# One set of products for the highest channel frequency, gates of the next FFN part ahead of a part's down products, and a prelude on zeros

## The chip, the cores and the metric

The kernel runs on 1 core of one Trainium2 chip. The metric is the device time of one execution in microseconds (us), as the median of several runs. The profile is that of one further execution.

## The reference

Two transformer blocks run one after the other on 512 tokens of 1024 channels, all in float32: a first block (FFN, a mixer with a recurrence over tokens, a second FFN), then a Fourier and attention layer, then a recurrent layer. Cut to what the change touches:

```python
def swiglu(x, w_gate, w_up, w_down):
    return (jax.nn.silu(x @ w_gate) * (x @ w_up)) @ w_down     # 1024 -> 2816 -> 1024

x = x + 0.5 * swiglu(rms_norm(x, ffn1_norm), ...)
x = x + token_mixer(...)
x = x + 0.5 * swiglu(rms_norm(x, ffn2_norm), ...)
...
# Fourier branch: 4 groups of 256 channels, real part of a 2-D transform over tokens and channels
fg = f_in.reshape(b, s, 4, 256)
fmix = jnp.fft.fftn(fg, axes=(1, 3), norm="ortho").real
fmix = jnp.einsum('bsgc,gce->bsge', fmix, fourier_w)
f_out = fmix * silu(f_gate)
```

## The kernel before

**Products.** Each float32 product is made of three TensorE products on fp32r halves: a high half and a low half of either operand (`mm3`, lines 783 to 787). Activations lie with channels on the partitions, so a tile is 128 channels x 512 tokens. A weight group (`wload`, line 732) is 512 KB: a DMA into one of three buffers `raw`, a cast into one of four `wh`, and on VectorE the difference into one of four `wl`; one group feeds 24 products of 512 columns for a depth of 1024.

**Low halves put aside.** During the two FFNs `put_low` (line 760) loads weights of a later stage as well, makes their low halves and writes these to DRAM; that stage then loads them (`wload_low`) instead of working them out. Two such groups go with each of the gates 0 to 19 and one with each down product of the first two parts.

**FFN** (`ffn`, line 855). The 2816 hidden channels are 22 tiles, in three parts of 8, 8 and 6. For a tile, here called a gate, there are a gate product and an up product (48 TensorE products), then `t = pg * rstd` on VectorE, Silu on ScalarE, `u = pu * rstd` on VectorE, `u * t` on GpSimd, and the split into halves `h`, `l`. When the gates of a part are done, eight down products sum over that part's tiles (24 TensorE products each, 18 in the last part) and are added to `x`. `rstd` comes from `rms` (line 844): the halves of `x`, and `sumsq` (line 807), in which ScalarE squares and GpSimd adds.

**Fourier branch** (`_even`, lines 1395 to 1453). For each of 4 groups: two input products, a transform over the 256 channels (129 cosines and 127 sines), sums and differences of token halves `s` and `d`, their splits, and then three token transforms by `seq`, each of 12 products of 256 columns: the cosines (`c1`), the sines (`c2`), and `pn`, the cosine transform of columns 128 to 255, of which only row 0, the highest channel frequency, is used (line 1435). Two gate products of the same group follow.

**Order.** The kernel is recorded, and a planner on the host (`Rec.schedule`, line 317) puts all instructions of all engines into one order by a list of costs. Each engine, and SyncE's DMA queue, then runs its part of that order strictly. An operation's priority is its place in the program plus `bias`; `late` (60) is the bias of the sum of squares. So moving a step in the program moves its loads, its put-aside weights and its evictions in every queue. All instructions carry line 555 in the profile, the line that issues them; the names of the tiles tell them apart.

Of the kernel before, what the change touches and what calls it, by code (L numbers as in the profile page):

```python
# [8 lines left out]
F32 = mybir.dt.float32  # L9
F32R = mybir.dt.float32r  # L10
AF = mybir.ActivationFunctionType
ALU = mybir.AluOpType
# [635 lines left out]
class Net:  # L648
    def __init__(self, tc, a, ctx, wbufs=(3, 4, 4), slots=76):
        self.tc, self.a = tc, a  # L650
        self.nc = self.rec = Rec(tc.nc)
        self.cp = ctx.enter_context(tc.tile_pool(name="cst", bufs=1))
        self.wp = ctx.enter_context(tc.tile_pool(name="wgt", bufs=1))
        self.wbufs = dict(zip(("raw", "wh", "wl"), wbufs))
        self.tp = ctx.enter_context(tc.tile_pool(name="act", bufs=1))
        self.sp = ctx.enter_context(tc.tile_pool(name="small", bufs=4))
        self.pm = ctx.enter_context(tc.tile_pool(name="pmm", bufs=8, space=PSUM))
        self.dp = ctx.enter_context(tc.tile_pool(name="dram", bufs=1, space=bass.MemoryType.DRAM))
        self.n = 0
        self.slots = slots  # L660
        self.late = 60
        self.low, self.later, self.behind, self.far = {}, [], 40, None
        nc = self.nc
        self.cst = self.cp.tile([128, _NC], F32, name="cst")
        self.vec = self.cp.tile([128, _NV], F32, name="vec")
        nc.sync.dma_start(out=self.vec, in_=a["vec"])
        self.load_x(a["xT"])
        nc.sync.dma_start(out=self.cst, in_=a["cst"])
        self.ident = self.c("ident")
        self.cr = {}  # L670
        for m in ("ones", "bones"):
            self.cr[m] = self.cp.tile([128, 128], F32R, name="r" + m)
            nc.vector.tensor_copy(self.cr[m], self.c(m))
        self.eps6 = self.cst[:, _COFF["eps"]:_COFF["eps"] + 1]
        self.epsg = self.cst[:, _COFF["eps"] + 1:_COFF["eps"] + 2]
        self.one = self.cst[:, _COFF["eps"] + 3:_COFF["eps"] + 4]
# [127 lines left out]
        self.nc.vector.scalar_tensor_tensor(l, src, g, h.bitcast(F32), op0=ALU.mult, op1=ALU.subtract)  # L804
        return h, l

    def sumsq(self, gains=None):

        nc = self.nc
        acc = self.T(p="acc")  # L810
        for k in range(KT):
            if k == 0:
                q = acc
            else:
                q = self.T(p="sq")
            if gains is None:
                nc.scalar.activation(q, self.x[k], AF.Square)
            else:
                nc.scalar.activation(q, self.x[k], AF.Square, scale=gains(k))
            if k:  # L820
                nc.gpsimd.tensor_tensor(acc, acc, q, ALU.add)
        ps = self.P()
        self.fold(ps, "ones", acc)
        return ps
# [16 lines left out]
        nc.vector.tensor_scalar(r, r, -0.5 * scale, 1.5, op0=ALU.mult, op1=ALU.add)  # L841
        nc.vector.tensor_tensor(out, out, r, ALU.mult)

    def rms(self, gname):

        xs = [self.split_scaled(self.x[k], self.v(gname, k)) for k in range(KT)]
        self.rec.bias = self.late
        ps = self.sumsq()
        rstd = self.T(p="rstd")
        self.rsqrt(rstd, ps, 1.0 / D, 1e-6)  # L850
        self.rec.bias = 0
        return xs, rstd


    def ffn(self, n):
        nc = self.nc
        xs, rstd = self.rms(n + "_norm")
        g0 = 0
        for ch, nk in enumerate((8, 8, 6)):
            hs = []  # L860
            for gi in range(g0, g0 + nk):
                wg = self.group(n + "_g", gi)
                pg = self.P()
                self.gemm(pg, wg, xs)
                wu = self.group(n + "_u", gi)
                pu = self.P()
                self.gemm(pu, wu, xs)
                t = self.T()
                nc.vector.tensor_tensor(t, pg, rstd, ALU.mult)
                nc.scalar.activation(t, t, AF.Silu)  # L870
                u = self.T()
                nc.vector.tensor_tensor(u, pu, rstd, ALU.mult)
                nc.gpsimd.tensor_tensor(u, u, t, ALU.mult)
                hs.append(self.split(u))
                if gi < 20:
                    self.put_low(2)
            g0 += nk
            for m in range(8):
                wd = self.group(f"{n}_d{ch}", m)
                ps = self.P()  # L880
                self.gemm(ps, wd, hs)
                xm = self.x[m]
                nc.vector.scalar_tensor_tensor(xm, ps, 0.5, xm, op0=ALU.mult, op1=ALU.add)
                if ch < 2:
                    self.put_low(1)


    def mixer(self):
# [457 lines left out]
    def _even(self):  # L1346
        nc = self.nc
        V, G, A, PE = nc.vector, nc.gpsimd, nc.scalar, nc.tensor
# [4 lines left out]
        xs = [self.split_scaled(x[k], g12[:, k:k + 1]) for k in range(KT)]  # L1353
# [4 lines left out]
        rstd = self.T(p="rs")  # L1358
# [25 lines left out]
        for gp in range(2):  # L1384
# [7 lines left out]
            V.tensor_copy(p[0:1], fwr[0:1, 0, gs])  # L1392
            V.tensor_copy(m[0:1], fwr[0:1, 1, gs])
            fw.append((p, m))
        fo = []
        for g in range(4):
            fs = []
            for m in range(2):
                w = self.group("e_f", 2 * g + m)
                ps = self.P()  # L1400
                self.gemm(ps, w, xs)
                f = self.T()
                V.tensor_tensor(f, ps, rstd, ALU.mult)
                fs.append(self.split(f))
            pp = []
            for tp in range(2):
                ps = self.P((128, 2, 256))
                for tt in range(2):
                    sl = slice((2 * tp + tt) * 128, (2 * tp + tt) * 128 + 128)
                    for k in range(2):  # L1410
                        self.mm3(ps[:, tt], fs[k][0][:, sl], fs[k][1][:, sl], d1h[:, k], d1l[:, k], k == 0, k == 1)
                pp.append(ps)
            b = self.T(shape=(128, 2, 256))
            A.copy(b, pp[1])
            s = self.T(shape=(128, 2, 256))
            d = self.T(shape=(128, 2, 256))
            V.tensor_tensor(s, pp[0], b, ALU.add)
            V.tensor_tensor(d, pp[0], b, ALU.subtract)
            sd = (self.split(s, (128, 2, 256)), self.split(d, (128, 2, 256)))

            def seq(col, tr):
                ps = self.P((128, 2, 256))
                for e in range(2):
                    h, l = sd[e]
                    for k in range(2):
                        self.mm3(ps[:, e], h[:, k, col], l[:, k, col], d2h[tr][e][:, k], d2l[tr][e][:, k], k == 0, k == 1)
                return ps
            c1, c2 = slice(0, 128), slice(128, 256)
            pc = seq(c1, 0)
            C = self.split(pc, (128, 2, 256))  # L1430
            pq = seq(c2, 1)
            Q = self.T(shape=(128, 2, 256))
            A.copy(Q, pq)
            pn = seq(c2, 0)
            V.tensor_copy(Q[0:1], pn[0:1])
            Qs = self.split(Q, (128, 2, 256))
            fl = lambda t: t.rearrange("p e j -> p (e j)")
            if g % 2 == 0:
                (ph, pl), (mh, ml) = [self.split(t, (128, 2, 256)) for t in fw[g // 2]]
            for m in range(2):  # L1440
                wg = self.group("e_f", 8 + 2 * g + m)
                pg = self.P()
                self.gemm(pg, wg, xs)
                sg = self.T()
                V.tensor_tensor(sg, pg, rstd, ALU.mult)
                A.activation(sg, sg, AF.Silu)
                po = self.P((128, 2, 256))
                ms = slice(m * 128, m * 128 + 128)
                self.mm3(fl(po), ph[:, g % 2, ms], pl[:, g % 2, ms], fl(C[0]), fl(C[1]), True, False)
                self.mm3(fl(po), mh[:, g % 2, ms], ml[:, g % 2, ms], fl(Qs[0]), fl(Qs[1]), False, True)  # L1450
                sv = sg.rearrange("p (j e) -> p e j", e=2)
                V.tensor_tensor(sv, sv, po, ALU.mult)
                fo.append(self.split(sg))
# [283 lines left out]
    def last_norm(self, hf):  # L1737
# [4 lines left out]
        s0 = slice(256 * hf, 256 * hf + 256)  # L1742
        if hf == 0:

            w = self.sm(1, tag="fw", bufs=1)
            o = A.activation(w, self.one, AF.Sqrt)
            o.deps.append(next(p for p in reversed(self.rec.ops[:-1]) if p.table))
        acc, q7 = (self.T(shape=(128, 512), p="sq")[:, 0:256] for _ in range(2))
# [31 lines left out]
    def all(self):  # L1780
# [2 lines left out]
        mix = [("w_in", t) for t in (5, 9, 1, 6, 10, 2, 7, 11, 3, 13, 17, 21, 14, 18, 22, 15, 19, 23, *range(26, 42))]  # L1783
        mix += [("w_out_a", h) for h in range(4)] + [("w_out_b", h) for h in range(4)] + [("w_o", g) for g in range(8)]
        n = len(self.rec.ops)
        self.later = mix
        self.ffn("ffn1")

        w = [o for o in self.rec.ops[n:] if o.fn == "dma_start"][:2]
        l = [o for o in self.rec.ops[:n] if o.fn == "dma_start"]  # L1790
# [31 lines left out]
```

## Time and profile before

| | us |
|---|---|
| Runs, median of 3 (lowest, highest) | 1879.77 (1878.92, 1880.1) |
| The profiled execution | 1883.26 |
| Its span, first to last instruction | 1881.5 |
| PE busy in the span | 1842.7 |
| DVE busy | 1272.1 |
| ACT busy | 852.2 |
| POOL busy | 246.4 |

PE is TensorE's products, PEld its weight loads, DVE VectorE, ACT ScalarE, POOL GpSimd, SPq SyncE's queue that issues the DMAs. A busy time of PE counts overlapping instructions once, and says nothing on how densely they follow each other: products of 512 columns are listed as 0.39 us long and start about 0.23 us apart. The rows therefore give counts beside the times. PEclk is the granted clock of TensorE as a share of 2.4 GHz; it has two levels, 2.4 and 1.2 GHz.

### The profile page before, as it was taken

The page shows a single profiled execution, that of the slowest core. Times are in us where ns is not written, and L with a number is a line of the kernel's source. Part 1 is how long each engine was busy: PE and PEld are TensorE (multiplying, and loading weights), DVE is VectorE, ACT ScalarE, POOL GpSimd, SP SyncE. Part 2 cuts the span into 40 slices and gives each one's busy share as a digit, 9 for nine tenths or more (in the row PEclk, how much of TensorE's full clock was granted, in tenths as well). Part 3 has the DMA queues.
Part 4 walks back from the last instruction along what each step waited for, and adds up shares of the span by engine and source line. Part 5 has one row for each costly group of instructions (what it writes and reads, how often), then busy time and mean ns, then how long its engine had stood idle before and what let it go on. Part 6 is the DMA issues. An engine that isn't in the chain of part 4 may idle for free.

```text
span 1881.5 us, 26365 instructions
## 1 busy us (share of the span) xinstructions
PE 1842.7 (98%) x10324; PEld 1540.2 (82%) x10324; DVE 1272.1 (68%) x1956; ACT 852.2 (45%) x1180; POOL 246.4 (13%) x193
## 2 busy tenths in 40 slices
PE   7999999999999999999998999999999999999998
PEld 6878878887788887888887887888999888888887
DVE  7766665579857434477467567965478965899773
ACT  5333433365324333444344335422255554998771
POOL 2101100113203002211010017010000010000001
PEclk9999999999999999999999999999999999999999
DMA  7788896445533444578788773322221125556552
GB/s 249 271 302 282 293 299 201 121 152 162 179 121 112 152 137 160 197 260 308 251 281 288 252 261 107 115 66 69 90 68 59 65 79 191 178 191 211 191 179 102
DMA packets 120398, 341.10 MB, mean 181 GB/s; under 512 B 33872, under 2 KB 36176, under 8 KB 120272
## 3 DMA queue, kind: packets, MB, share of 16 engines
q1 hardware_dynamic: 120272, 339.41, 54.0%
q8 instruction: 81, 1.33, 0.3%
q14 instruction: 45, 0.37, 0.1%
HBM read 277.76 MB, written 61.60 MB: 180 GB/s over the span
## 4 chain that ended last, share of the span: by engine, by line
PE 73%; DMA 11%; DVE 11%; ACT 3%; issue 2%; POOL 0%; SPq 0%; DVEq 0%; ACTq 0%; POOLq 0%
PE pm L555 69%; DVE wl L555 5%; PE pw L555 4%; DMA low<-wl 2%; DMA raw<-o_in 2%; ACT wh L555 2%; DVE t L555 2%; DMA raw<-ffn_d 1%; DMA raw<-ffn_u 1%; DVE l L555 1%; DMA raw<-gw 1%; DMA raw<-w_in 1%; DMA raw<-w_out_a 1%; DVE wh L555 0%; DVE u L555 0%
## 5 line engine op out<-in xcount | busy, mean ns | idle before, releaser
L555 ACT CAST wh<-raw 128x1024 fp32r<-128x1024 f32 (+1 forms) x334 | 347.1, 1041 | 687.6 <-PE pm L555 278.4
L555 PE MATMUL pm<-xh,wh 128*128 128x512 f32 x1488 | 583.1, 392 | 8.4 <-ACT xh L555 8.2
L555 PE MATMUL pm<-xl,wh 128*128 128x512 f32 x1488 | 582.0, 391 | 2.5 <-DVE xl L555 2.5
L555 PE MATMUL pm<-xh,wl 128*128 128x512 f32 x1488 | 582.3, 391 | 1.1 <-DVE wl L555 1.0
L555 DVE TENSOR_TENSOR wl<-raw,wh 128x1024 fp32r<-128x1024 f32 (+1 forms) x302 | 386.3, 1282 | 202.2 <-DMA low<-wl 92.0
L555 PEld LDWEIGHTS pm<-xh,wh 128*128 128x128 f32 x1488 | 280.3, 188 | 67.2 <-ACT xh L555 9.4
L555 PEld LDWEIGHTS pm<-xl,wh 128*128 128x128 f32 x1488 | 280.4, 188 | 62.5 <-DVE xl L555 5.2
L555 PEld LDWEIGHTS pm<-xh,wl 128*128 128x128 f32 x1488 | 280.2, 188 | 60.5 <-DVE wl L555 2.8
L555 PE MATMUL pm<-h,wh 128*128 128x512 f32 (+1 forms) x832 | 319.1, 386 | 9.6 <-ACT h L555 9.0
L555 PE MATMUL pm<-l,wh 128*128 128x512 f32 (+1 forms) x832 | 319.9, 385 | 1.1 <-DVE l L555 1.1
L555 PE MATMUL pm<-h,wl 128*128 128x512 f32 (+1 forms) x832 | 319.5, 385 | 1.4 <-DMA wl<-low 1.2
L555 POOL TENSOR_TENSOR t<-t,t 128x512 f32<-128x512 f32 x60 | 88.8, 1481 | 932.1 <-DVE t L555 712.5
L555 PEld LDWEIGHTS pm<-h,wh 128*128 128x128 f32 x832 | 157.4, 190 | 42.8 <-ACT h L555 10.5
L555 PEld LDWEIGHTS pm<-l,wh 128*128 128x128 f32 x832 | 157.9, 190 | 33.7 <-DVE l L555 3.5
L555 PEld LDWEIGHTS pm<-h,wl 128*128 128x128 f32 x832 | 157.8, 190 | 32.1 <-DMA wl<-low 1.6
L555 DVE TENSOR_TENSOR t<-pm,rstd 128x512 f32<-128x512 f32 x146 | 98.8, 685 | 22.1 <-PE pm L555 17.6
L555 ACT ACT_TABLE_LOAD x71 | 91.1, 1283 | 24.8 <-DVE s L555 15.7
L555 DVE CAST wh<-raw 128x1024 fp32r<-128x1024 f32 x74 | 53.9, 728 | 58.2 <-PE pm L555 31.1
L555 POOL TENSOR_TENSOR acc<-acc,sq 128x512 f32<-128x512 f32 x42 | 66.2, 1584 | 140.0 <-ACT sq L555 139.7
L555 DVE TENSOR_TENSOR x<-x,pm 128x512 f32<-128x512 f32 (+1 forms) x44 | 27.9, 637 | 72.5 <-PE pm L555 70.4
L555 ACT ACTIVATE t<-t 128x512 f32<-128x512 f32 x100 | 59.7, 626 | 21.7 <-DVE t L555 20.1
L555 DVE TENSOR_TENSOR l<-t,h 128x512 fp32r<-128x512 f32 x87 | 61.0, 709 | 6.9 <-ACT h L555 5.5
(251 smaller groups left out, 2040.1 us busy)
## 6 DMA issues: line engine op xcount, KB each, us to landing
low<-wl SPq DMA_DIRECT2D x106, 512.0 KB, 3.8
wl<-low SPq DMA_DIRECT2D x106, 512.0 KB, 3.5
raw<-w_in SPq DMA_DIRECT2D x76, 512.0 KB, 4.7
raw<-o_in SPq DMA_DIRECT2D x64, 512.0 KB, 4.5
raw<-ffn_g SPq DMA_DIRECT2D x44, 512.0 KB, 4.4
raw<-ffn_u SPq DMA_DIRECT2D x44, 512.0 KB, 5.1
raw<-ffn_d SPq DMA_DIRECT2D x32, 512.0 KB, 5.1
raw<-o_out SPq DMA_DIRECT2D x32, 512.0 KB, 4.5
```

The source lines that it names most:

```text
L555: o.ins = getattr(getattr(self.nc, o.eng), o.fn)(*o.args, **o.kw)
```

## The change

There are four edits.

- Before anything else a tile `z` is zeroed on GpSimd, ScalarE takes a square root of one of its columns, and TensorE multiplies `z` by itself 20 times (128x512) into a tile that nobody reads. The tag of a one-column tile in `last_norm` is renamed so that it has a buffer of its own.
- In the first FFN, the seven additions of the sum of squares go from GpSimd to VectorE, and the bias of that sum from 60 to 100.
- In both FFNs, gate 8 comes ahead of the eight down products of the first part, gate 16 ahead of the first six of the second part, and the other two of the second part come behind gate 21, ahead of those of the third part.
- In the Fourier branch, all four groups go through input products, channel transform and splits first. Column 128 of each group's halves is copied into columns 0, 32, 64 and 96 of two zeroed tiles `ny`, and 12 products on these give `pn` for all groups at once; ScalarE copies it to SBUF. The other two token transforms and the gates follow group by group.

```diff
@@ Net.__init__ @@
+        z = self.T(F32R, p="z")
+        nc.gpsimd.memset(z.bitcast(F32), 0.0)
+        nc.scalar.activation(self.sm(1, tag="fw", bufs=1), z[:, 0:1].bitcast(F32), AF.Sqrt)
+        ps = self.P()
+        for _ in range(20):
+            nc.tensor.matmul(ps, z[:, 0:128], z, start=True, stop=True)
@@ sumsq @@
-                nc.gpsimd.tensor_tensor(acc, acc, q, ALU.add)
+                getattr(nc, adds).tensor_tensor(acc, acc, q, ALU.add)
@@ ffn @@
-        xs, rstd = self.rms(n + "_norm")
-        g0 = 0
-        for ch, nk in enumerate((8, 8, 6)):
-            hs = []
-            for gi in range(g0, g0 + nk):
...
-            for m in range(8):
-                wd = self.group(f"{n}_d{ch}", m)
...
+        xs, rstd = self.rms(n + "_norm", "vector" if n == "ffn1" else "gpsimd")
+        hs = [[], [], []]
+        def gate(gi):
...
+        def down(ch, m):
...
+        for gi in range(22):
+            gate(gi)
+            if gi in (8, 16):
+                for m in range(8 if gi == 8 else 6):
+                    down(gi // 8 - 1, m)
+        for m in (6, 7):
+            down(1, m)
+        for m in range(8):
+            down(2, m)
@@ _even @@
+        nyq = [self.T(F32R, (128, 2, 2, 128), "ny") for _ in range(2)]
+        for t in nyq:
+            G.memset(t.bitcast(F32), 0.0)
+        sds = []
         for g in range(4):
...
+            for e in range(2):
+                for t, hl in zip(nyq, sd[e]):
+                    nc.copy(t[:, e, :, 32 * g:32 * g + 1], hl[:, :, 128:129])
+            sds.append(sd)
+        ps = self.P((128, 2, 256))
+        for e in range(2):
+            for k in range(2):
+                self.mm3(ps[:, e], nyq[0][:, e, k], nyq[1][:, e, k], d2h[0][e][:, k], d2l[0][e][:, k], k == 0, k == 1)
+        pn = self.T(shape=(128, 2, 256), p="pn")
+        A.copy(pn, ps)
+        fo = []
+        for g in range(4):
             def seq(col, tr):
...
-            pn = seq(c2, 0)
-            V.tensor_copy(Q[0:1], pn[0:1])
+            V.tensor_copy(Q[0:1], pn[32 * g:32 * g + 1])
@@ last_norm @@
-            w = self.sm(1, tag="fw", bufs=1)
+            w = self.sm(1, tag="fx", bufs=1)
@@ all @@
+        late, self.late = self.late, 100
         self.later = mix
         self.ffn("ffn1")
+        self.late = late
```

## Rows read from the trace of the kernel before

**Rows 1.** Page, part 1: busy us, share of the span, instructions.

```profile
PE 1842.7 (98%) x10324; PEld 1540.2 (82%) x10324; DVE 1272.1 (68%) x1956; ACT 852.2 (45%) x1180; POOL 246.4 (13%) x193
```

**Rows 2.** Stretches: us, busy time (xcount), PEclk, DMA share, GB/s.

```profile
0.00:21.00 21.00, 11.13 (x32) 7.15 (x33) 13.62 (x14) 13.29 (x20) 8.17 (x10) 1.00 0.73 263
106.00:118.00 12.00, 9.46 (x29) 6.90 (x28) 8.10 (x9) 4.71 (x5) 1.28 (x1) 0.72 0.90 307
118.00:243.00 125.00, 125.00 (x553) 103.56 (x552) 83.96 (x89) 46.01 (x48) 14.65 (x9) 1.00 0.85 291
243.00:248.00 5.00, 3.60 (x15) 2.42 (x14) 3.23 (x5) 3.41 (x4) 0.00 (x0) 1.00 0.72 265
1015.00:1030.00 15.00, 9.14 (x27) 6.64 (x27) 10.16 (x11) 5.78 (x7) 1.26 (x1) 0.77 0.91 305
1180.00:1400.00 220.00, 220.00 (x1251) 193.29 (x1250) 139.35 (x212) 75.56 (x103) 14.98 (x14) 1.00 0.25 83
```

**Rows 3.** Timeline of PE, first 21 us: start, length, operation, wait.

```profile
8.23 0.79 PE L555 MATMUL pm<-xh,wh 128*128 128x512 f32 x1 [8.23 <-ACT xh L555]
...
14.38 0.40 PE L555 MATMUL pm<-xl,wh 128*128 128x512 f32 x1
...
20.83 0.50 PE L555 MATMUL pm<-xl,wh 128*128 128x512 f32 x1 [1.17 <-DVE xl L555]
```

**Rows 4.** Timeline of ACT, first 21 us.

```profile
6.17 1.28 ACT L555 ACT_TABLE_LOAD   x1 [6.17 <-DMA x<-xT]
```

**Rows 5.** Timeline of DVE, first 27 us.

```profile
5.32 0.69 DVE L555 CAST wh<-raw 128x1024 fp32r<-128x1024 f32 x1 [5.32 <-DMA raw<-ffn_g]
6.05 1.22 DVE L555 TENSOR_TENSOR wl<-raw,wh 128x1024 fp32r<-128x1024 f32 x1
...
9.35 0.75 DVE L555 SCALAR_TENSOR_TENSOR xl<-x,vec,xh 128x512 fp32r<-128x512 f32 x1 [0.38 <-ACT xh L555]
...
12.25 5.46 DVE L555 SCALAR_TENSOR_TENSOR xl<-x,vec,xh 128x512 fp32r<-128x512 f32 x5
...
20.70 5.67 DVE L555 TENSOR_TENSOR wl<-raw,wh 128x1024 fp32r<-128x1024 f32 x3
```

**Rows 6.** Timeline of POOL at 242 us, the one memset of this size.

```profile
241.96 0.53 POOL L555 MEMSET z<- 128x512 f32 x1
```

**Rows 7.** Timeline of PE around 107 us, where gates end.

```profile
109.09 0.73 PE L555 MATMUL pm<-h,wh 128*128 128x512 f32 x2 [1.92 <-ACT h L555]
...
115.72 0.63 PE L555 MATMUL pm<-h,wl 128*128 128x512 f32 x1
116.15 0.62 PE L555 MATMUL pm<-h,wh 128*128 128x512 f32 x1
```

**Rows 8.** Timeline of ACT at the same place.

```profile
106.20 1.05 ACT L555 CAST wh<-raw 128x1024 fp32r<-128x1024 f32 x1 [2.46 <-DMA raw<-ffn_d]
...
108.43 0.61 ACT L555 CAST h<-t 128x512 fp32r<-128x512 f32 x1
```

**Rows 9.** Timeline of DVE around 1019 us, second FFN, second part.

```profile
1018.76 0.68 DVE L555 TENSOR_TENSOR t<-pm,rstd 128x512 f32<-128x512 f32 x1
...
1021.95 0.69 DVE L555 TENSOR_TENSOR l<-t,h 128x512 fp32r<-128x512 f32 x1
```

**Rows 10.** Timeline of PE, second FFN, where gates of the second part end.

```profile
1021.97 0.79 PE L555 MATMUL pm<-h,wh 128*128 128x512 f32 x1 [5.86 <-ACT h L555]
```

**Rows 11.** Chain that ended last, first 112 us: start, length, what.

```profile
53.84 5.21 DMA raw<-ffn_u
...
76.19 5.07 DMA raw<-ffn_u
```

**Rows 12.** Timeline of PE, Fourier branch, products of 256 columns.

```profile
1207.26 0.28 PE L555 MATMUL pm<-h,l 128*128 128x256 f32 x1
...
1210.72 0.28 PE L555 MATMUL pm<-h,l 128*128 128x256 f32 x1
```

**Rows 13.** DVE groups, 1180 to 1400 us: shape, count, busy, mean ns.

```profile
L555 DVE COPY t<-pm 1x512 f32<-1x512 f32 x4 | 2.7, 678 | 3.4 <-PE pm L555 3.4
```


## What was predicted

> **What bounds the kernel now.** I read the page's busy times first: PE is busy 1842.7 of 1881.5 us, no other engine over 68% [rows 1]. A busy PE can still be slow, so I counted products by stretch next; in those rows the first bracket is PE's count, and the last three values are PEclk, DMA share and GB/s [rows 2]. From 118 to 243 us 553 products of 512 columns start in 125.00 us: 0.226 us each. I take this as PE at its peak and price every stretch by it; what is over is time that an edit can give back. Three kinds of place show an excess:
>
> - The first 21 us: 32 products are 7.2 us of work, so 13.8 us are lost. The timeline of PE tells why: the first product starts at 8.23 and lasts 0.79, at 14.38 one lasts 0.40. So the engine is idle for 8.2 us, on the lower of its two levels for about 6 us after its first product, and at the end waits for `xl` [rows 3].
> - The ends of the gates of a part. 106 to 118 us: 29 products, 6.55 us of work in 12, 5.4 lost. 243 to 248: 15 products, 1.6 lost. 1015 to 1030, in the second FFN: 27 products, 8.9 lost [rows 2]. PE waits there for the split of the last gate's tile (`<-ACT h`), 1.92 and 5.86 us [rows 7, 10], and then goes at the lower level: starts 0.43 us apart, PEclk 0.72 and 0.77 over the stretches [rows 2, 7].
> - In the Fourier branch there is none: PE is busy 220.00 of 220.00 us from 1180 to 1400, DVE 139, ACT 76 [rows 2]. Time is gained there only by fewer products.
>
> **The change, part by part.** The sum is made against the profiled execution, 1883.3 us (1881.5 of span and 1.8 around it); it is 3.5 us over the median of the runs, and I carry the difference over to the median.
>
> *Prelude on zeros.* The memset costs POOL 0.53 us [rows 6], so the 20 products can start at about 1.2 us. No row shows a prelude; the nearest is the first stretch, where the level rose about 6 us after the first product [rows 3]. By it 14 products go 0.43 us apart (7.2 us by the clock) and six at 0.226 (1.4), and the first real product starts at 8.5, at the upper level. It was 8.23 before, so the idle time stays and what goes is the slow part: 8.5 us lost instead of 13.8, 5.3 gained. The square root pulls the table load of 1.28 us, which waited for the first DMA of `x` and held up the first `xh` [rows 4], into idle time; behind the prelude this is worth nothing. If the level rises at once, the first real product can start at 8.23 - 1.28 = 6.95 and 6.8 us are gained; if it doesn't rise in the prelude, PE is taken until 1.2 + 20 x 0.43 = 9.8, 1.6 us later than before, and 1.6 is lost.
>
> *Additions to VectorE.* While GpSimd adds, VectorE's own work is stretched: five `xl` take 5.46 us, against 0.75 for a lone one; three `wl` 5.67, against 1.22 for a lone one [rows 5]. The seven additions at 0.69 us, the length of a difference of the same size [rows 9], cost VectorE 4.8 us ahead of the next weights. VectorE's work until the third of these `wl`: 1.9 for the first weights, eight `xl` at 0.75, a second `wl` 1.2, additions 4.8, three `wl` 3.7, with two small casts some 18 us from 5.3: 23.3 if nothing else makes it idle, where it was 26.4 [rows 5]. So the weights come 3.1 us earlier, PE 5.3. The weights have nothing to spare: the second down weight of the first part, eighteen groups on, is cast from 106.20 to 107.25, and PE had done with the first one at 107.17 [rows 7, 8]. The start is therefore worth between 3.1 (stream without slack) and 5.3. I take 4.0, ends -1.6 and 6.8 from above.
>
> *Gates between gates and down products.* Removed: the wait for the last gate's split. In its place PE has another gate, 48 products or 10.9 us, and then the 21 products of a down product that don't need the last tile, 4.8 us: 15.6 us of cover. What has to fit: from the end of the last up product to the end of `l`. At the worst end that product's end lies 21 products ahead of the stall: 1021.97 - 5.86 - 0.2 - 4.75 = 1011.2; `t` left PSUM only at 1018.76, because VectorE's strict order held it behind `wl`, and `l` ended at 1022.6 [rows 9, 10]: 11.5 us, under the cover. With each moved gate go its two weight loads, two put-aside groups with their writes, and its evictions, ahead of eight (six) down weights on SP's queue and VectorE. Per PE time a gate and two down products ask the same of both: 3.1 MB of DMA per 10.9 us, 289 GB/s at 0.524 MB a transfer. The trace holds 291 GB/s at a DMA share of 0.85 with PE at its peak for 125 us [rows 2]. So I count 1.5 of 1.6, 8.5 of 8.9, and at the first end, where the weights too were late, 4.0 of 5.4: 14.0. Ends: 9.5 (the first end gives nothing, 0.5 more stays at each of the others) and 16.
>
> The Trainium skill's page "TensorE: Matmul & The Clock Gate" (HAM oscillation) warns of idle gaps, but only of longer ones than the 1.92 us here. By it the first end would have cost its 1.9 us of idle time alone, and the forecast would be 2.1 us later; the rows show the lower level there [rows 2, 7], so the measurement decides.
>
> *One set for the highest frequency.* Four sets of 12 products of 256 columns become one: 36 fewer. Thirty of them in a row start from 1207.26 to 1210.72, 0.119 us apart [rows 12]: 4.3 us off a busy PE. Added: 16 copies of one column per half, which no row shows. They cost no more than the one-row copy of 512, 0.68 us [rows 13], so 0 to 10.9 us, on VectorE and ScalarE, which are idle for 81 and 144 us in the stretch [rows 2]; two memsets of 0.53 on POOL and one copy on ScalarE are covered alike. Without the cover, the last group's copies (four, 2.7 us) would stand ahead of `pn`; but PE then has all other token transforms and gate products to do. The row copies stay. I take 4.2, ends 1.6 (4.3 less those 2.7) and 4.3.
>
> *All else.* The planner orders everything anew. The rest of the kernel keeps its work; I count 0, with 4 us on either side (about half of the 8.9 us stall).
>
> Sum: 4.0 + 14.0 + 4.2 = 22.2. 1883.3 - 22.2 = 1861.1 by the profile's measure, 1879.8 - 22.2 = 1857.6 by the median.
>
> **Rivals.**
>
> - *The weights set the pace of the FFNs*, and the stalls were their time to catch up. For: the chain runs through a DMA of `raw` once a gate from 53.84 to 76.19, 11.2 us a gate where PE needs 10.9 [rows 11]. 44 gates at 0.3 are 13 us back. Against: 125 us at the peak [rows 2]. Time: 1857.6 + 13 = 1871, PE waiting for `wh` or `wl` in many small gaps.
> - *The prelude doesn't do what it says*: the level stays low until real products have run. Start -1.6 instead of 4.0: 1863.
> - *Slower: evictions come too late everywhere.* In the new order a whole gate's `wl`s stand ahead of the last gate's `t` in VectorE's queue, as they did at 1018.76. It decides from 15.6 us between up product and split (11.5 was the worst). Then all six ends of parts cost 8.9: 53 us instead of the 16 of now. 1879.8 + 37 - 8.2 = 1909.
>
> **How the numbers follow.** Forecast 0.62, weights 0.22, prelude 0.08, evictions 0.08. The forecast's low end takes the best of each term and a lucky order: 6.8 + 16 + 4.3 + 4 = 31, 1849. The high end reaches to the weights' rival, 1872. About 0.2% (3.8 us) can be told from no change. Slower: the evictions and little else, 0.08. Same: the weights' rival with the low ends of start and set, 0.05. Faster: 0.87.
>
> **What would show it.** Start: a first real product near 8.5 us that lasts 0.4, and the 48th done near 20 to 21 us. Ends of parts: no `<-ACT h` wait over 1 us in either FFN, PEclk 1.00 throughout. Weights' rival: waits for `wl` or `wh` in the gates, or fewer than 440 products per 100 us. Fourier: 12 products on `ny`, 36 fewer of 256 columns, PE still without a gap. Wrong would be a new stall with PEclk at half in the mixer, or a count below the peak in the FFNs.

## The result, and the profile after

| | before | after |
|---|---|---|
| Median of the runs, us (lowest, highest) | 1879.35 (1877.19, 1880.1) | 1866.3 (1861.76, 1866.88) |
| The profiled execution | 1883.26 | 1866.76 |
| Its span | 1881.5 | 1864.9 |

The ratio of the medians is 0.993, with an interval of 0.9913 to 0.9946: faster by 13.1 us, where 22.2 were forecast. The median lies in the range (1849 to 1872), 8.7 us above the forecast of 1857.6. By the profiled executions it is 16.5 us, against the same forecast of 22.2.

First the stretches of the changed kernel that answer to [rows 2]; columns as there (the first bracket is PE's count of instructions, then PEld, DVE, ACT, POOL; the last three values are PEclk, DMA share, GB/s).

```profile
0.00:21.00 21.00, 19.10 (x70) 14.27 (x71) 14.35 (x21) 14.68 (x22) 0.73 (x5) 1.00 0.74 264
105.00:118.00 13.00, 13.00 (x59) 10.78 (x58) 7.96 (x8) 5.70 (x7) 1.30 (x1) 1.00 0.88 306
140.00:170.00 30.00, 25.79 (x110) 20.05 (x109) 13.43 (x14) 8.40 (x8) 0.00 (x0) 1.00 0.71 228
243.00:248.00 5.00, 5.00 (x24) 4.14 (x23) 4.21 (x6) 2.35 (x3) 0.15 (x1) 1.00 0.95 349
925.00:965.00 40.00, 37.90 (x165) 30.42 (x164) 23.91 (x26) 14.16 (x15) 3.42 (x2) 1.00 0.76 249
1005.00:1022.00 17.00, 17.00 (x76) 14.08 (x76) 11.26 (x14) 8.44 (x9) 1.28 (x1) 1.00 0.92 318
1055.00:1065.00 10.00, 9.28 (x41) 7.34 (x40) 5.26 (x6) 3.79 (x4) 0.00 (x0) 1.00 0.74 227
1170.00:1390.00 220.00, 220.00 (x1264) 194.17 (x1263) 143.00 (x229) 80.16 (x127) 14.45 (x14) 1.00 0.24 80
```

Read them against 0.226 us per product, as the prediction did.

- **The start.** Of the 70 products of the first 21 us 20 are the prelude, so 50 are real; before there were 32 [rows 2]. 18 x 0.226 = 4.1 us gained.
- **The old stalls are gone.** At 105 to 118, 243 to 248 and 1005 to 1022 us PE is at its peak (59, 24 and 76 products, where 57.5, 22 and 75 fit) and PEclk is 1.00. The 5.4, 1.6 and 8.9 us of [rows 2] are gained in full: 15.9.
- **There are new losses where none was before.** From 140 to 170 us 110 products begin where 132.7 fit: 5.1 us lost. From 925 to 965 it is 165 of 177, 2.7 us; from 1055 to 1065, 41 of 44, 0.7 us. Together 8.5.
- **The Fourier branch** keeps PE busy 220.00 of 220.00 us, as before, and has 36 products of 256 columns fewer, 4.3 us by [rows 12].

4.1 + 15.9 - 8.5 + 4.3 = 15.8 of the 16.6 us between the spans; 0.8 are in none of these places. All this is one execution of either kernel, and the new losses are not the same each time: in the profile of the changed kernel once more (further down) they are 2.6, 0.7 and 0.5 us at these places and 1.4 more behind 170 us, together 5.2.

What the new losses are, the waits of PE say. These rows are of the changed kernel, for 0 to 345 us (the first FFN) and 800 to 1130 us (the second): what PE waited for, us in total, times, the longest.

```profile
PE pm L555 <- DVE wl L555: 4.2, 4, 1.3
...
PE pm L555 <- DVE wl L555: 2.8, 4, 1.2
```

No wait for a split (`<-ACT h`) is left in either FFN; before it was 1.92 us at the first end and 5.86 in the second FFN [rows 7, 10], and 1.18 at 245 us. In their place PE waits for low halves of weights. PE's timeline has three of the first four, and the chain of work that ended last, from 146 to 169 us, shows what holds them up (start, length, what):

```profile
154.57 0.50 PE L555 MATMUL pm<-xh,wl 128*128 128x512 f32 x1 [1.20 <-DVE wl L555]
...
161.60 0.50 PE L555 MATMUL pm<-xh,wl 128*128 128x512 f32 x1 [1.28 <-DVE wl L555]
...
168.64 0.50 PE L555 MATMUL pm<-xh,wl 128*128 128x512 f32 x1 [1.31 <-DVE wl L555]
```

```profile
147.51 0.68 DVE x L555
148.19 1.14 DVE wl L555
149.33 0.02 issue
149.35 3.82 DMA low<-wl
...
153.29 1.24 DVE wl L555
...
162.15 1.14 DVE wl L555
163.31 3.93 DMA low<-wl
...
167.36 1.24 DVE wl L555
168.60 0.04 issue
168.64 1.43 PE pm L555 x5
```

A put-aside group takes one of the four `wl`. Its write to DRAM (`low<-wl`) takes 3.8 to 3.9 us, and only when it has landed can the next `wl` that PE needs be written into the same buffer, at 153.29 and 167.36. PE waits for those at 154.57 and 168.64. Between them, at 161.60, it waits for a `wl` begun at 160.32, which the chain puts down to a cast that was over 0.94 us before; a put-aside write issued at 156.28 would land at about 160.2 if it took the same 3.9 us (an estimate). So PE waits every 7.0 us, where 24 products take 24 x 0.226 = 5.4. The engines are not full meanwhile: DVE is busy 13.43 of the 30 us, the DMA share is 0.71. That points to a ring of waits over four buffers rather than a lack of bandwidth. The chain between 154 and 162 us also passes a load into `raw` (3.70 us) that began when the `wl` of 153.29 was done, so by itself it doesn't rule the loading out; the experiments do that.

The ring is not a steady pace of this kernel. Behind the new losses PE is at its peak again with the same four buffers (324 products, where 323 fit):

```profile
170.00:243.00 73.00, 73.00 (x324) 60.28 (x323) 48.04 (x54) 31.08 (x33) 12.85 (x7) 1.00 0.84 289
```

Why it closes at these places and not at others isn't shown.

### The profile page after: what moved, and what is told of

Its sections match the earlier page's. It is cut to its first block, busy times and chain, and to the rows that moved or that the text cites. A ratio compares the mean times of both kernels' runs of the same rounds, so it can differ in the third digit from the quotient of the medians.

```text
span 1864.9 us, 26367 instructions
## 1 busy us (share of the span) xinstructions
PE 1836.5 (98%) x10308; PEld 1535.8 (82%) x10308; DVE 1262.5 (68%) x1958; ACT 858.4 (46%) x1202; POOL 246.5 (13%) x189
## 4 chain that ended last, share of the span: by engine, by line
PE 68%; DMA 15%; DVE 10%; ACT 3%; issue 2%; POOL 1%; SPq 1%; DVEq 0%; ACTq 0%; POOLq 0%
PE pm L555 64%; DMA low<-wl 6%; DVE wl L555 6%; PE pw L555 4%; DMA raw<-o_in 2%; ACT wh L555 2%; DMA raw<-w_in 2%; DVE t L555 1%; DMA raw<-gw 1%; DMA raw<-ffn_d 1%; DMA raw<-ffn_u 1%; DMA raw<-o_out 1%; DVE l L555 1%; SPq L555 1%; DMA raw<-ffn_g 0%
## 5 line engine op out<-in xcount | busy, mean ns | idle before, releaser
L555 DVE TENSOR_TENSOR wl<-raw,wh 128x1024 fp32r<-128x1024 f32 (+1 forms) x302 | 381.3, 1264 | 203.4 <-DMA low<-wl 92.9
L555 POOL TENSOR_TENSOR t<-t,t 128x512 f32<-128x512 f32 x60 | 98.5, 1643 | 898.9 <-DVE t L555 689.9
L555 POOL TENSOR_TENSOR acc<-acc,sq 128x512 f32<-128x512 f32 x35 | 55.4, 1592 | 149.3 <-ACT sq L555 149.3
```

The costliest lines, as they stand in the source:

```text
L555: o.ins = getattr(getattr(self.nc, o.eng), o.fn)(*o.args, **o.kw)
```

## The experiments

All of them were run beside the kernel before on the same chip, whose median was 1877.89 (the first four), 1877.99 (the next four) and 1877.15 us (the last four); a chip's own difference is taken against that. The theories: that the start's lead is given back to the weight stream, so that the order alone gives nearly as much as the whole; that what limits the stream is the four `wl`, held by put-aside writes; and as rivals, that it is the loading (`raw`), the DMA bandwidth, or the put-aside groups as such. What a name or letter in a quoted expectation stands for is told there.

**The new order alone** (`ffn` of the changed kernel; no prelude, additions on GpSimd, old Fourier branch):

```diff
-        xs, rstd = self.rms(n + "_norm", "vector" if n == "ffn1" else "gpsimd")
+        xs, rstd = self.rms(n + "_norm")
```

> The kernel before with the new FFN order alone (no prelude, additions on GpSimd, bias 60, four sets for the highest frequency). In the changed kernel the order took 18.3 us of waits for the split out of the span and put 9.9 us of new waits, mostly for wl, in, at 140 to 170 and at 925 to 965 us. Theory A (the new waits come because PE now runs ahead of its weight stream, and a PE that starts 4 us later has 4 us more slack in the first FFN): the wl waits of the first FFN fall from 5.3 to 1 to 2 us, those of the second stay near 4; span 12 us below the 1881.5 of before, about 1869. Theory B (the waits belong to the order itself, whenever PE starts): 5 us of them stay in the first FFN; span near 1873, 8 us below before.

Measured: 1866.48 us, ratio 0.994 (0.9927 to 0.9954), so 11.4 of the 13 to 16 us that the whole change gives. How its first FFN stands to that of the whole shows in the count of products begun by 140, 243 and 345 us. The order alone:

```profile
0.00:140.00 140.00, 129.77 (x554) 105.08 (x555) 105.21 (x104) 58.08 (x72) 24.86 (x20) 1.00 0.80 275
0.00:243.00 243.00, 232.77 (x1009) 190.39 (x1010) 175.88 (x179) 97.58 (x113) 34.72 (x27) 1.00 0.82 283
0.00:345.00 345.00, 334.14 (x1455) 274.01 (x1456) 235.76 (x253) 128.06 (x147) 43.76 (x34) 1.00 0.77 264
```

The whole change, whose first 20 are the prelude:

```profile
0.00:140.00 140.00, 137.98 (x593) 112.36 (x594) 105.28 (x113) 60.63 (x75) 17.55 (x14) 1.00 0.83 284
0.00:243.00 243.00, 236.77 (x1024) 192.68 (x1025) 166.75 (x180) 100.11 (x116) 30.40 (x21) 1.00 0.82 279
0.00:345.00 345.00, 338.77 (x1473) 277.04 (x1474) 228.77 (x256) 131.63 (x151) 39.58 (x28) 1.00 0.78 263
```

At 140 us the whole is 573 - 554 = 19 products ahead, 4.3 us: the start's gain, intact. At 243 us it is 1004 - 1009 = 5 behind, at 345 us 2 behind. The start's lead is all given back between 140 and 243 us, in the waits for `wl`; the order alone, which comes to that place 4.3 us later, waits 0.6 us for `wl` in this FFN and not at all in the second. Two more kernels of this order with four `wl` (both further down) give the lead back at the same place: the changed kernel once more is 23 products ahead at 140 us and 3 at 243, that with 74 tiles 18 ahead and then 5 behind. So Theory A is right for the first FFN. For the second it isn't: the expectation had about 4 us of waits there for the order alone, and there is none (so its span, 1864.4 us, is below those of both theories). The waits of the second FFN vary (2.8 us in the whole change, 1.0 in its repetition, 0.3 with 74 tiles), and since the whole is level with the order alone at 345 us, the start's lead doesn't explain them; their cause is open.

**The single set alone** (the changed `_even`, nothing else):

```diff
-            pn = seq(c2, 0)
-            V.tensor_copy(Q[0:1], pn[0:1])
+            V.tensor_copy(Q[0:1], pn[32 * g:32 * g + 1])
```

> The kernel before with the Fourier edit alone. 36 products of 256 columns fewer at 0.119 us: 4.3 us off the span if PE sets the pace of the branch throughout, ratio about 0.998; PE loses under 1 us to waits between 1180 and 1400 us. Rival: the 16 column copies or the later splits hold the token transforms up, and 1 us or less is gained.

Measured: 1874.16 us, ratio 0.9977 (0.9966 to 0.9987), 3.7 us faster. The interval (2.4 to 6.4 us) holds the 4.2 of the forecast. In the changed kernel the set and its copies look thus (groups by shape, 1160 to 1400 us: count, busy us, mean ns, idle time before them):

```profile
L555 PE MATMUL pm<-h,ny 128*128 128x256 f32 x8 | 1.6, 280 | 0.0
L555 ACT CAST ny<-h 128x2 fp32r<-128x2 f32 x8 | 1.4, 192 | 0.2 <-DVE h L555 0.2
```

A copy of one column for both token halves takes 0.19 us. I had bounded it by 0.68, and nothing hung on it.

**The start alone**, and **the prelude alone** (the additions stay on GpSimd, the bias at 60):

```diff
+        z = self.T(F32R, p="z")
...
-        xs, rstd = self.rms(n + "_norm")
+        xs, rstd = self.rms(n + "_norm", "vector" if n == "ffn1" else "gpsimd")
...
+        late, self.late = self.late, 100
```

> The kernel before with the start alone: prelude, additions of the first sum on VectorE, bias 100. By 25 us PE should be 4 us ahead of before. Theory A (the weight stream of the first FFN has about 1 us of slack and decides at the first end of a part): of the 4 us 2 to 3 are left at 250 us, and the end near 107 us costs more than the 5.4 of before. Theory B (the lead is kept): 4 us off at 250 us and off the span, and the end near 107 us costs as before.

> The kernel before with the prelude on zeros alone; GpSimd still adds. If the clock's level is what the start loses, PE is 3.5 to 4.5 us ahead at 25 us as with the additions moved too. If GpSimd's additions beside VectorE hold back the xl and wl, the gain stops at 1 to 2.5 us, since at 20.83 us PE waited for xl before.

Measured: the start 1876.11 us, ratio 0.9989 (0.9975 to 1.0002); the prelude 1876.85 us, 0.9992 (0.9979 to 1.0005). Neither can be told from no change; but the intervals (from 0.4 us slower to 4.7 faster, and from 0.9 slower to 3.9 faster) don't rule out the gains of the first 21 us either. There the start alone begins 70 products, the whole of its 4.1 us, and the prelude alone 58: 38 real ones, 1.4 us more than before. This is the prelude alone, the beginning of PE's timeline and the stretch:

```profile
1.31 7.70 PE L555 MATMUL pm<-z 128*128 128x512 f32 x20 [1.31 <-POOL z L555]
8.85 0.39 PE L555 MATMUL pm<-xh,wh 128*128 128x512 f32 x1
...
0.00:21.00 21.00, 17.48 (x58) 12.61 (x59) 14.27 (x14) 14.18 (x22) 9.36 (x11) 1.00 0.74 263
```

So a third of the start's gain comes from the prelude, and two thirds come when the additions leave GpSimd and their place becomes later as well; the additions without the prelude were not run. Where the gates of the first part end, PE of the start alone waits longer than before (1.92 us [rows 7]) for the same split, but that doesn't take the lead. From 100 to 118 us 50 products begin, before 51, and by 243 us the start alone has begun 1016 - 20 = 996 real products where before began 981, 15 more or 3.4 us. First the kernel before, then the start alone:

```profile
0.00:243.00 243.00, 230.37 (x981) 187.16 (x982) 174.29 (x177) 96.62 (x112) 38.55 (x28) 0.99 0.81 280
```

```profile
0.00:243.00 243.00, 236.30 (x1016) 193.35 (x1017) 173.50 (x186) 100.77 (x117) 29.70 (x22) 0.99 0.83 286
```

That is nearer to Theory B of the expectation (the lead is kept) than to A, though in one execution, the fastest of eleven; by the median the start alone is 1.8 us faster. Its longer wait, and a later one:

```profile
106.58 0.79 PE L555 MATMUL pm<-h,wh 128*128 128x512 f32 x1 [4.17 <-ACT h L555]
...
1012.56 0.50 PE L555 MATMUL pm<-h,wh 128*128 128x512 f32 x1 [1.11 <-ACT h L555]
```

The second of these two is the place of the worst stall before, 5.86 us [rows 10]. Three kernels that keep the old order of the FFNs wait there 1.11 (the start alone), 1.58 (the prelude alone) and 4.76 us (the single set alone). So the stall is not a constant of the order.

**The changed kernel once more, and three edits of its weight stream**: a fifth `wl` (with 74 tiles of 128x512 instead of 76, to make room), a fourth `raw` instead (likewise), and no put-aside groups with the down products of the first part.

> The changed kernel once more. The ends of parts cost very different amounts from one execution to the next in the kernels with the old order (8.9 us at the second FFN's second part before, 2 to 6 us with single edits). If the wait for wl near 146 to 168 us comes from the order and the start, it stands again, 4 to 6 us, and the lead at the 48th product (9.7 us lost by then) is gone by the 1500th (16 lost). If it is chance of that execution, it is under 2 us.

```diff
-    def __init__(self, tc, a, ctx, wbufs=(3, 4, 4), slots=76):
+    def __init__(self, tc, a, ctx, wbufs=(3, 4, 5), slots=74):
```

> The changed kernel with five wl buffers for four, and 74 activation tiles for 76 to make room. Theory W (put-aside halves hold wl until they are written to DRAM, and the next wl of the FFN's own weights waits for it): the waits of PE for wl near 150 us fall from 5.3 to under 1 us, time 4 to 8 us lower, near 1860. Theory R (the raw buffers or their loads set the pace): no change in these waits. Theory D (DMA rate): no change either, DMA share above 0.85 in the stretch.

```diff
-    def __init__(self, tc, a, ctx, wbufs=(3, 4, 4), slots=76):
+    def __init__(self, tc, a, ctx, wbufs=(4, 4, 4), slots=74):
```

> The changed kernel with four raw buffers for three, and 74 activation tiles. Theory R (loads wait for a free raw): waits for wl near 150 us under 1 us, time near 1860. Theory W (wl held by put-aside writes): the waits stay at 4 us or more.

```diff
-            if ch < 2:
+            if ch == 1:
                 self.put_low(1)
```

> The changed kernel without the put-aside groups that go with the down products of the first part, in both FFNs; the eight last groups of each list make their low halves in their own stage instead. This takes the writes away where the waits are. Theory W: no wait for wl between 140 and 170 us and none of over 0.5 us between 925 and 965; time 3 to 8 us lower, less what the later stages pay. Theory R: loads are fewer as well, so the waits fall too, and only the two runs with more buffers tell W and R apart. A third cause (VectorE's own time): little change, VectorE is busy 13.4 of 30 us there.

Measured: the changed kernel 1861.99 us, ratio 0.992 (0.9907 to 0.9933); five `wl` 1855.37, 0.9881 (0.9869 to 0.9894); four `raw` 1899.1, 1.011 (1.0097 to 1.0123); fewer put-aside groups 1893.04, 1.0083 (1.007 to 1.0096).

In the changed kernel once more the waits for `wl` stand at the same place, but smaller than expected: 3.0 us in the first FFN (the expectation had 4 to 6, or under 2 if it was chance), and 121 products from 140 to 170 us instead of 110. The place is that of the order and the start; the size varies.

The stretch from 140 to 170 us with five `wl`:

```profile
140.00:170.00 30.00, 30.00 (x134) 24.85 (x133) 18.71 (x19) 13.05 (x14) 1.29 (x1) 1.00 0.91 307
```

PE is at its peak, no wait for `wl` is left in either FFN, and the DMA share rises from 0.71 to 0.91: the same weights, the same writes, 307 GB/s instead of 228. Bandwidth was there; the buffer was missing. The start's lead over the order alone is kept as well: 23 products at 140 us, 22 at 243 and 26 at 345. A fourth `raw` doesn't help but harms: PE waits for `wl` 15 times in the first FFN and 17 in the second (the row is of the whole kernel). At the old place the ring is the same: PE waits at 151.24, 158.22 and 165.13 us, 7.0 us apart, and the `wl` of 156.94 had waited 4.02 us for a put-aside write (`low<-wl`):

```profile
PE pm L555 <- DVE wl L555: 30.9, 33, 1.7
...
151.24 0.50 PE L555 MATMUL pm<-h,wl 128*128 128x512 f32 x1 [1.37 <-DVE wl L555]
...
158.22 0.50 PE L555 MATMUL pm<-xh,wl 128*128 128x512 f32 x1 [1.22 <-DVE wl L555]
```

So it isn't the loading that holds PE up there. Why more `raw` make it so much worse isn't shown by a run; that groups loaded earlier take `wl` out of turn would fit, but I didn't separate it from the different plan.

The kernel with fewer put-aside groups was meant to free the ring at its place, and did: 134 products from 140 to 170 us, at a DMA share of 0.44. But the list of groups is worked off in order, so what isn't put aside there comes later. At 337 us the ring closes again, and PE loses more than it won:

```profile
330.00:360.00 30.00, 18.71 (x61) 14.10 (x60) 11.85 (x15) 0.00 (x0) 1.29 (x1) 0.82 0.32 109
```

The chain there (start, length, what) begins like the other, with PE at its end:

```profile
337.60 1.24 DVE wl L555
338.84 0.02 issue
338.85 2.83 DMA low<-wl
...
341.78 1.24 DVE wl L555
343.02 0.04 issue
343.06 8.06 PE pm L555 x22
```

Two writes stand in it, of 2.83 and 2.92 us; from 364 us on it goes through loads into `raw` instead, so only its first part shows the mechanism at a second place. At 400 us this kernel is 114 products behind the changed one, about 26 of the 31 us between their medians. Ten groups fewer are put aside (96 writes instead of 106: two fewer in the first FFN, eight in the second); what these ten cost in their own stages isn't separated from the later place of the others.

**Controls**: 74 tiles alone; the kernel before with five `wl`; five `wl` and the new order without the start; and five `wl` with one more edit, the first sum of squares of the Fourier layer on VectorE.

> The changed kernel with 74 activation tiles for 76 and nothing else, the control of the runs with one buffer more. If the fifth wl buffer did it, the waits for wl near 150 us stand (3 to 6 us) and the time is that of the changed kernel, 1861 to 1867. If the planner's other order with 74 tiles did it, it is near 1855.

```diff
-    def __init__(self, tc, a, ctx, wbufs=(3, 4, 4), slots=76):
+    def __init__(self, tc, a, ctx, wbufs=(3, 4, 4), slots=74):
```

> The kernel before with five wl buffers and 74 tiles: old FFN order, no prelude, four sets. The late evictions at the ends of parts stood behind wl that waited for a put-aside write. Theory A (the fifth buffer alone takes most of that wait away): ends of parts cost 2 to 6 us in all instead of 16, time 1866 to 1872. Theory B (the split's own length decides, so the order is needed): 8 us or more stay, time above 1872.

```diff
 (in the kernel before)
-    def __init__(self, tc, a, ctx, wbufs=(3, 4, 4), slots=76):
+    def __init__(self, tc, a, ctx, wbufs=(3, 4, 5), slots=74):
```

> Five wl buffers, new FFN order and Fourier edit, without the prelude, with additions on GpSimd and bias 60. Theory (the start's 4 us are kept when the weight stream has slack): 4 us over the run with five buffers and the start, 1859 to 1860, with 14 us lost by the 1500th product of the first FFN instead of 9.7. Rival (the start counts nothing over the whole kernel): 1855 to 1857.

```diff
 (with five wl)
-        z = self.T(F32R, p="z")
...
-        xs, rstd = self.rms(n + "_norm", "vector" if n == "ffn1" else "gpsimd")
+        xs, rstd = self.rms(n + "_norm", "gpsimd")
...
-        late, self.late = self.late, 100
```

> Five wl buffers and the whole change, with the seven additions of the Fourier layer's first sum of squares on VectorE too. In the run with five buffers PE loses 7 us near 1146 us, most of it in a 3.4 us wait for the split of that sum and the lower level behind it. If GpSimd's additions (1.6 us each, twice seven) set that wait, it shrinks to under 2 us and the time falls by 2 to 5 us, near 1852. If the last weights or x set it, nothing changes.

```diff
 (with five wl, in _even)
-        s1 = self.sumsq()
+        s1 = self.sumsq(adds="vector")
```

Measured:

| | median, us | ratio (interval) |
|---|---|---|
| 74 tiles alone | 1863.67 | 0.9926 (0.9913 to 0.9938) |
| before with five `wl` | 1870.22 | 0.996 (0.9948 to 0.9973) |
| five `wl`, without the start | 1862.47 | 0.9919 (0.9905 to 0.9932) |
| five `wl`, sum on VectorE | 1852.94 | 0.987 (0.9856 to 0.9883) |

74 tiles change nothing: the stretch from 140 to 170 us is that of the changed kernel.

```profile
140.00:170.00 30.00, 26.25 (x113) 20.41 (x112) 13.63 (x14) 8.40 (x8) 0.00 (x0) 1.00 0.72 229
```

A fifth `wl` in the kernel before (with 74 tiles, which were not run there by themselves) takes 6.9 us off: there too buffers delayed the splits, for in the second FFN PE of this kernel waits for nothing, and at the end of the first part 0.93 us instead of 1.92. With five `wl` the start is worth 1862.47 - 1855.37 = 7.1 us by medians that stand on two chips (0.0038 by the ratios, the same); with four it could not be told from none. That is more than the 4 expected. The other way round, a fifth `wl` without the start gives nothing that the medians show: 14.7 us, where the order alone and the set alone give 11.4 + 3.7 = 15.1. Of the 7.1 us, 4.1 are the start itself. The rest stands at 118 us of the profile without the start, where the weights run short:

```profile
118.59 0.50 PE L555 MATMUL pm<-h,wh 128*128 128x512 f32 x1 [0.77 <-ACT wh L555]
...
120.11 0.50 PE L555 MATMUL pm<-h,wl 128*128 128x512 f32 x1 [0.79 <-DVE wl L555]
...
121.23 0.63 PE L555 MATMUL pm<-h,wh 128*128 128x512 f32 x1
```

From 110 to 125 us 51 products begin where 66.4 fit, 3.5 us lost. With the start 40 low halves have been begun by 118 us, without it 36, and this wait isn't there.

The last kernel is the fastest seen. Its gain over five `wl` alone, 2.4 us by medians of two chips, isn't told apart by the intervals, which overlap; the stretch from 1130 to 1165 us shows it, though, first with five `wl`, then with the sum on VectorE as well:

```profile
1130.00:1165.00 35.00, 30.13 (x121) 23.51 (x120) 30.28 (x29) 18.79 (x27) 21.88 (x12) 0.90 0.38 129
```

```profile
1130.00:1165.00 35.00, 32.52 (x135) 26.11 (x134) 32.69 (x34) 19.91 (x28) 14.79 (x8) 0.95 0.43 149
```

14 more products begin, about 3 us. The wait for the split of that sum, 3.27 us with five `wl`, is gone, as expected if GpSimd's additions set it; two waits for weights, of 1.38 and 1.10 us, stand ahead of it instead.

## Why the prediction was right and wrong

**What bounds the kernel**: right. The time came from the places that the counts had shown, and nowhere else to speak of.

**The start**: right in size, 4.1 us by the count against 4.0, for a partly wrong reason. I took the clock to rise 6 us after the first product and the first real product to begin at 8.5. In the changed kernel it begins at 7.85:

```profile
1.31 6.70 PE L555 MATMUL pm<-z 128*128 128x512 f32 x20 [1.31 <-POOL z L555]
7.85 0.39 PE L555 MATMUL pm<-xh,wh 128*128 128x512 f32 x1
```

But that decides little. In the kernel with 74 tiles it begins at 8.80 and 70 products have begun by 21 us, the same number. VectorE's chain decides, for which my working had a bound of 3.1 us, and the additions were the larger part of it. The step that failed is what follows: "the weights have nothing to spare" was said of the start, and its conclusion, that PE's lead is worth only what the stream can follow, was not carried on to 140 us, where the whole 4 us went with four `wl` in the new order.

**The ends of the gates**: the term was mis-sized, 14.0 forecast, 15.9 - 8.5 = 7.4 found. The first half was right: the wait for the last split is gone at every end, the first one included (I counted 4.0 of its 5.4), the cover was enough, and PEclk is 1.00. The step that failed is "a gate and two down products ask the same of both: 3.1 MB of DMA per 10.9 us". That compares rates, and the rates do suffice, as the 307 GB/s with five `wl` show. It leaves out for how long a transfer holds its buffer, 3.8 us of a write in which one of four `wl` is lost to PE. The peak from 118 to 243 us, on which I leant [rows 2], came behind a stall of 5.4 us that had let the stream get ahead; the order alone, 4.3 us behind the whole, and the peak behind the new losses fit that. The trace of before had a sign of it: the `wl` ahead of the late `t` of 1018.76 [rows 9], which I put down to VectorE's strict order alone, had itself waited for a put-aside write.

```profile
1017.61 1.23 DVE L555 TENSOR_TENSOR wl<-raw,wh 128x1024 fp32r<-128x1024 f32 x1 [1.85 <-DMA low<-wl]
```

With the 5.2 us of losses in the repetition the term would be 10.7, so part of the miss is the chance of one profiled execution.

**The Fourier set**: right, 4.3 us by the count and 3.7 (2.4 to 6.4) by itself.

**All else at 0**: 0.8 in the profile. The order alone, the set alone and the start alone add up to 11.4 + 3.7 + 1.8 = 16.9 us, against 13.1, 16.0 and 13.5 for the whole in three comparisons (the last with 74 tiles).

**From the profile to the median**: I carried a difference of 3.5 us over, as if it were the same for both kernels. It wasn't: after, the profiled execution is 0.5 us over its median. The runs of the kernel before spread, from 1873.32 to 1884.21 us in the 27 of the first comparison, and the wait of 5.86 us [rows 10], of which I counted 8.5 us as gain, was 1.11 to 4.76 in three relatives. That this one stall was long in the profiled execution, and so the gain by the median smaller than by the profile, fits; no run shows it for before itself.

So of the 8.7 us by which the median is above the forecast, 6.6 are the term of the ends (14.0 - 7.4), 3.0 the carried profile (3.5 - 0.5), and 0.9 of the other terms goes the other way.

**The rivals.** The weights as the pace came partly true, 8.5 us instead of 13, at the buffer that I had not named; I had looked at `raw` [rows 11]. I gave it 0.22. Right was its sign, gaps at `wl` in the gates; they stand in three places and not in all 44 gates. The prelude does what it says, but alone is worth 1.4 us by 21 us. Evictions too late: no trace of it, no `<-ACT h` wait in either FFN.

## What to carry to other kernels

Beside the bytes per time of a stream, count its buffers: each is taken from the first write into it until the last reader is done, a write-back to DRAM among these, and the sum of these times over the number of buffers can be a pace of its own. Here it was one for some 20 us at a time and not throughout. A stall can hide it, since the stream gets ahead meanwhile; so when a stall is removed, ask which buffer is late next, and whether the rows at full speed came right behind a stall. A single profiled execution of a kernel with stalls is one draw: before a stall of 6 us is priced, look whether relatives of the kernel show it as long.

## What the runs showed of the hardware

- **The same prelude of 20 products takes 6.21 to 7.70 us** in nine profiles. At 0.43 us apart on the lower level and 0.227 on the upper, the 19 steps of the changed kernel (6.31 us from first to last start) hold about 10 slow ones, the 7.31 us of the prelude alone about 15: by this estimate the clock rose about 4 us after the first product in the one, 6 in the other. I had expected one value, 6.
- **Short waits can be followed by the lower level, or not.** Two waits of 0.77 and 0.79 us, 1.5 us apart, were followed by products 0.43 us apart from 121.23 to 124.22 us (PEclk 0.89 from 110 to 125 us, five `wl` without the start); waits of 1.20 and 1.28 us, 7.0 us apart, in the changed kernel weren't (PEclk 1.00 from 140 to 170 us). The Trainium skill's page "TensorE: Matmul & The Clock Gate" (HAM oscillation) tells of longer gaps alone; the first case speaks against resting on that, as the 1.92 us did before.
- **A further buffer can cost time**: a fourth `raw` made the kernel 1.1% slower than before and 2% slower than the changed kernel. The planner's order changed with it, and the two weren't separated.
